# More rooms for prefetched expert weights, two output-projection chunks loaded early in both layers, and the recurrence's tables ordered behind the first norm

## The chip, the cores and the metric

The kernel runs on one core of a Trainium2 chip. The metric is the device time of one execution in microseconds (us); lower is better. Engines are called by the profile's short names: PE (TensorE), PEld (its weight loads), DVE (VectorE), ACT (ScalarE), POOL (GpSimd) and SP (SyncE, which here issues almost all loads).

## The reference, cut to what matters

Two layers over 512 tokens of width 1024: 256 latent tokens and 256 context tokens. Only the latent tokens are needed at the end, so layer 1 computes its queries, merge and experts for 256 tokens.

```python
h = modulate(rms_norm(x), shift, scale)        # shift, scale, gate = (silu(c) @ ada_w + ada_b)
parts = project(h, w_in)                       # attention, S5, HGRN, and 3*1024 gate logits
y_att, y_s5, y_hg = diff_attention, s5 recurrence, hgrn recurrence
g = sigmoid(gate_logits)                       # (3, 1024)
m = g[0]*(y_att @ w_o_att) + g[1]*(y_s5 @ w_o_s5) + g[2]*(y_hg @ w_o_hg)
x = x + gate1 * (m @ w_out)
h2 = modulate(rms_norm(x))
x = x + gate2 * hier_moe(h2)                   # 32 experts, top 2 in one of 4 groups
# one expert: (silu(xb @ w_gate[e]) * (xb @ w_up[e])) @ w_down[e]
```

An S5 recurrence needs tables, powers of its complex decay, that depend on the weights alone.

## The kernel before, in words

Each layer has three stages, and one scheduler (it keeps a model of the engines' time and fixes, before the run, the order of instructions on each engine) puts them in order.

**Dense** (`dense`): the norm and its modulation (`norm_mod`, lines L332 to L344) write the transposed activations as two parts `hTh` and `hTl`; `w_in` comes in chunks of 1 MB (`wchunk`, L159, tiles `wst`), each is split by ACT (`wh`, L364) and DVE (`wl`, L367), and a product is three matmuls (L347 to L349). Results go to DRAM: the gates as `dg` (12 blocks), the branches' outputs as `dy`. In layer 0 the stage begins with the modulation vector: `ada_step` (L264) multiplies chunks of `ada_w` into `adaP`, `ada_end` adds a bias on DVE (L270, `stg`), turns the result on PE (L273) and copies it to `mod` (L276), which the norm's modulation needs. `s5_prep` computes the S5 tables (tiles `p_a`, `p_b`, `p_w`, `p_e`, `p_cu`, `p_u`, `p_t`, `p_pw`; L213 to L218 are the complex multiplication `cmul`, L563 to L565 the drive table), mostly on DVE; L584 and L596 are the S5 matmuls on PE that use them.

**Merge**: for each branch the output comes back from DRAM (`yf`, L1299), is split (`yh` on ACT, L729, `yl` on DVE, L730), and is multiplied by its `w_o` chunk in four column blocks; each block is multiplied by its gate (`gt`, L1316, from `dg`) and added up in `mTl`. S5 comes first, HGRN second, attention last. Then `w_out` in four chunks, c = 0 to 3, each a column block: the product, `m_w` (L1351, times the gate), and the add to `Xx`/`Xctx` (L1354), and the router's share of those columns. In both layers w_out's chunks come through the four rooms `wp`, which the `w_o` chunks hold before; in layer 1 the chunks 2 and 3 go to two of the rooms `xw` instead (the list `Wo`).

**Experts** (`expert_rows`): 32 experts in 192 chunks of 1 MB per layer (`mgate`, `mup`, `mdown`: 64 each), always in one order. Each chunk takes the next room of a list, `self.slots`: the `xw` rooms (7 in layer 0, 11 in layer 1, in the space that `hTh` and `hTl` leave), the 4 `wp`, and the rooms `xt` (4 in each layer, one of them in layer 0 opened late as `NXU`). `prefetch` (L189) issues the load on SP; where it is called in merge, a one-element DVE copy (L184) into the room ties it to a step: `PM` says how many follow each of merge's 12 column blocks, `PF` how many follow the first `m_w` of each w_out chunk, `PRE` how many before the router's count is read back. SP then reads that count (`v_n`, L1769) and branches (L1770). In layer 0 a pass computes two experts for two token halves (12 chunks, 16 groups); in layer 1 four experts (24 chunks, 8 groups). `pg`, `pu`, `py` are the three products (L1627); `cw` (L1753, DVE) weights a result and POOL adds it to the tokens (L1755).

All loads on SP's queue are issued in order: an item whose room is not free holds back those behind it.

Of the kernel before, what the change touches and what calls it, by code (L numbers as in the profile page):

```python
# [13 lines left out]
OP = mybir.AluOpType  # L14
# [6 lines left out]
LEVELS = (64, 32, 16, 8, 4, 2, 1)  # L21
SCAN_ORD = list(range(31, -1, -1)) + list(range(63, 31, -1))
NE = 32
NXW = (7,11)
NXT = (4,4)
PRE = (3,0)
NXU = (1,0)
ORDER = ((0, 8, 9, 7, 10, 11, 1), (0, 8, 9, 7, 10, 11, 1))
SHARE = (0, 3)
ATT1 = (0, 0)  # L30
PM = ((0,0,0,0,0,0,1,1,1,1,1,0),(0,0,0,0,0,0,0,0,1,1,1,1))
PF = ((0,0,1,2),(2,3,3,0))

ROWS = 32

# [91 lines left out]
class Trunk:  # L127
# [35 lines left out]
    def stream_begin(self, l):  # L163
        self.nxw = NXW[l]
        self.xw = self.mes.enter_context(self.tc.tile_pool(name=f"mw{l}", bufs=self.nxw, side="right"))
# [159 lines left out]
    def norm_mod(self, l, Z, R, hi, lo, pool):  # L325

        nc = self.nc
        g = pool.tile([128, 8], FT, name="nmg")
        nc.scalar.dma_start(g, self.h["nmix"][l])
        a = pool.tile([128, 8, 2], FT, name="nma")  # L330
        m = self.mod[l]
        nc.vector.scalar_tensor_tensor(a, m[:, 8:16, :], 1.0, g[:, :, None].to_broadcast([128, 8, 2]), op0=OP.add, op1=OP.mult)  # L332
        for j in range(8):
            T = Z[:, j]
            if R is not None:
                T = pool.tile([128, 512], FT, name="nzr", bufs=2)
                nc.vector.tensor_mul(T, Z[:, j], R)
            f = pool.tile([128, 512], FT, name="nf", bufs=2)
            nc.scalar.activation(f[:, 0:256], T[:, 0:256], AF.Identity, bias=m[:, j, 1:2], scale=a[:, j, 1:2])
            nc.vector.tensor_scalar(f[:, 256:512], T[:, 256:512], a[:, j, 0:1], m[:, j, 0:1], op0=OP.mult, op1=OP.add)  # L340
            nc.scalar.copy(hi[:, j, :], f)  # L341
            (nc.gpsimd if j % 2 else nc.vector).tensor_sub(lo[:, j, :], f, hi[:, j, :].bitcast(FT))


# [153 lines left out]
    def s5_prep(self, l, ps, ne):  # L498

        nc, tc, h = self.nc, self.tc, self.h  # L500
        V, G = nc.vector, nc.gpsimd
        store = (nc.sync if l == 0 else nc.scalar).dma_start
        with ExitStack() as es:
# [5 lines left out]
            nc.sync.dma_start(dd, h["s5d"][l])  # L509
            if l == 0:  # L510
                yield from self.s5_setup(pool)
            else:
                yield
            T = self.s5t[l]
            C, P, F = self.s5s[l]

# [559 lines left out]
    def dense(self, l):  # L1076
        nc, tc, h = self.nc, self.tc, self.h
# [4 lines left out]
        es = ExitStack()  # L1082
# [20 lines left out]
        if l == 0:  # L1103
            self.cond_vectors(ap)
            self.s5k = ap
            with ExitStack() as ns:
                npool = ns.enter_context(tc.tile_pool(name=f"nrm{l}", bufs=1))
                X = npool.tile([128, 4, D], FT, name="nx")
                ada = self.ada(0, 0, ap)
                next(ada)  # L1110
                for t in range(NT):
                    nc.sync.dma_start(X[:, t], h["x" if t > 1 else "ctx"][128 * (t % 2):128 * (t % 2) + 128])
                next(ada)
                pre = self.s5_prep(l, ps, 2)
                next(pre)
                with tc.high_priority():
                    turned = self.norm_rows(l, [X[:, t] for t in range(NT)], npool, acc)
                    for _ in ada:
                        pass
                    self.norm_mod(l, *turned, hi, lo, npool)  # L1120
                for _ in pre:
                    pass
        if l == 0:
            def rest():
                for a, g in ((0, 1), (0, 2), (1, 0), (1, 1), (1, 2)):
# [118 lines left out]
        pre = self.s5_prep(1, ps, 1) if l == 0 else iter(())  # L1244
# [31 lines left out]
        ls.close()  # L1276
        clear()

        Wo = {c: self.wchunk(h["w_out"][l, c], self.xw) for c in ((2, 3) if l else ())}
        self.slots = self.slots[len(Wo):] + self.slots[:len(Wo)]  # L1280
        with ExitStack() as ss:
            mp = ss.enter_context(tc.tile_pool(name=f"mrh{l}", bufs=1))
# [5 lines left out]
            with ExitStack() as s2:  # L1288
                yp = s2.enter_context(tc.tile_pool(name=f"yp{l}", bufs=1, side="right" if l == 0 else "left"))
                yi = s2.enter_context(tc.tile_pool(name=f"yi{l}", bufs=2, side="right" if l == 0 else "left"))  # L1290
                for bi, (b, prs) in enumerate(((1, (2,)), (2, (3,)), (0, (0, 1)))):
                    Y, W = {}, {}
                    for p in prs:
                        if p == 2 and ys5:
                            Y[p] = [[t[:, k] for t in ys5] for k in range(2)]
                        else:
                            m = 1 if p == 1 and ya3 else 2
# [6 lines left out]
                    for q in range(4):  # L1304
# [29 lines left out]
                            nc.sync.dma_start(t, h[n].rearrange("(t p) d -> p t d", p=128))  # L1334
                        for _ in range(PM[l][4 * bi + q]):
                            self.prefetch(m_[:, 0] if one else m_)
            self.router_begin(l, ps, pa)
            for c in range(4):
                P = [bank() for _ in range(nq // 2)]
# [16 lines left out]
                        for _ in range(PF[l][c]):  # L1356
                            self.prefetch(w[:, 0])
                self.router_cols(l, c)
            while self.taken < self.nxw + 4:
                self.prefetch()  # L1360
            self.sp = [t for t in self.sp if t is self.sp0]
            with tc.high_priority():
# [5 lines left out]
    def router_begin(self, l, ps, pl):  # L1368

        nc, h = self.nc, self.h  # L1370
# [9 lines left out]

        rp = self.rp = self.rts.enter_context(self.tc.tile_pool(name=f"rt{l}", bufs=1, side="right"))
        rk = lambda nm, *sh: rp.tile([128, *sh], FT, name=nm)
        self.constants(rp, "route", nc.gpsimd)
        wr, br, gc = rk("r_w", 8, 36), rp.tile([1, 36], FT, name="r_b"), rk("r_g", 8)
        nc.sync.dma_start(wr, h["wr"][l])
        nc.sync.dma_start(br, h["br"][l:l + 1])
# [2 lines left out]
        m = self.mod[l]  # L1389
# [3 lines left out]
        for r in rs:  # L1393
            a = self.rc[r] = self.mp.tile([128, 8], FT, name=f"r_c{r}")
# [134 lines left out]
    def moe(self, l, rs):  # L1529
        nc, tc, h = self.nc, self.tc, self.h  # L1530
# [3 lines left out]
        es = ExitStack()  # L1534
# [9 lines left out]
        ng, m = NE // na, na * nq  # L1544
        self.g2 = {r: self.mod_bc(mp, l, 5, r, f"g2_{r}") for r in ((0, 1) if l == 0 else (0,))}

        xt = es.enter_context(tc.tile_pool(name=f"mx{l}", bufs=NXT[l] - NXU[l]))
        self.slots += [xt] * (NXT[l] - NXU[l])
        self.slots = self.slots[self.taken % len(self.slots):] + self.slots[:self.taken % len(self.slots)]
        for _ in range(PRE[l]):  # L1550
            self.prefetch()
# [10 lines left out]
            return OH  # L1562
        first = picked(0)
        self.router_rows(l, rs, 1)
        if NXU[l]:
            xt = es.enter_context(tc.tile_pool(name=f"my{l}", bufs=NXU[l]))
            self.slots = [xt] * NXU[l] + self.slots
        self.m2 = es.enter_context(tc.tile_pool(name=f"mo2{l}", bufs=2))
        self.ot = self.m2.tile([128, nt * 128], FR, name="ot", bufs=1)
        def gather(q, OH, part=None):  # L1570

# [11 lines left out]
        if l:  # L1583
            nxt = gather(0, first)
        for _ in range(NXT[l] - PRE[l]):
            self.prefetch(self.X[x0])
# [3 lines left out]
        for p in range(ng):  # L1590
# [18 lines left out]
            with self.in_order(), tc.high_priority() if last else nullcontext():  # L1609
                back = self.expert_rows(*cur[p % nq], na, self.ns, W, last, before, behind)  # L1610
                for f in back if last else ():
                    f()
        es.close()
        self.mes.close()

    @contextmanager
# [58 lines left out]
    def expert_rows(self, xT, sl, na, ns, W, last=False, before=lambda: None, behind=lambda: None, later=True):  # L1675
# [4 lines left out]
        nc = self.nc  # L1680
# [31 lines left out]
        for i, (c0, m) in enumerate(((0, 512), (512, 256), (768, 256)) if last else ((0, 512), (512, 512))):  # L1712
            n, c1 = divmod(c0, 512)
            cut = lambda t: t[:, 0:m]
            Y = cut(self.py.tile([128, 2, 256], FT, name="py").rearrange("p a n -> p (a n)"))
            for k in range(4):
                for a in range(ng):
                    self.pe(nc.tensor.matmul, Y[ps_[a]], hT[:, k, ps_[a]], part(W[4 + n][a % na], k)[:, c1:c1 + m], start=k == 0, stop=k == 3)
            whole = last and m < 512
            yh = cut(self.parts("wh", FT if whole else FR))  # L1720
            S.activation(yh, Y, AF.Identity, scale=sl[:, 0:1])  # L1721
            if not whole:
                yl = cut(self.parts("wl"))
                V.scalar_tensor_tensor(yl, Y, sl[:, 0:1], yh.bitcast(FT), op0=OP.mult, op1=OP.subtract)
            back.append(lambda c0=c0, m=m, yh=yh, yl=None if whole else yl, i=i: self.expert_back(c0, m, yh, yl, ns, last, i))
            if not later or last and i:
                back.pop(0)()
# [125 lines left out]
```

## Time and profile before

| | us |
|---|---|
| median of 3 runs | 2017.79 (2015.47 to 2020.94) |
| the profiled execution, its own time | 2008.41 |
| its span in the profile | 2006.7 |
| PE busy | 1745.2 (87%) |
| DVE busy | 1036.7 (52%) |
| ACT busy | 534.3 (27%) |
| POOL busy | 506.5 (25%) |
| mean granted TensorE clock | 0.947 |

The stages, by the start of their first matmuls: dense of layer 0 from 43, merge from 541.8, w_out about 590 to 647, router to 678, experts to about 1143; dense of layer 1 to about 1489 (its merge begins at about 1473), w_out 1497 to 1530, router, and experts from 1548.4 to the end. Shares of busy time over the whole span hide that the stages have different limits, so the stages are read one by one.

### The profile page before, as it was taken

What the parts mean: (1) busy time and instruction counts of PE and PEld (TensorE: products, weight loads), DVE (VectorE), ACT (ScalarE), POOL (GpSimd) and SP (SyncE); (2) the same over time, 40 slices, a digit from 0 to 9 for tenths busy, and PEclk for the clock granted to TensorE, in tenths of its full rate; (3) what the DMA queues carried; (4) which work ended last, traced back from release to release, by engine and by line L of the source; (5) the groups of instructions that cost most, each with busy time, mean ns of one, the idle gap of its engine ahead of it and who ended that gap; (6) DMA issues with size and microseconds to landing.
All of it is one profiled execution on the core that took longest, in us unless ns stands there. A gap on an engine that the chain in (4) does not pass through costs nothing. (4 is left out here: it accounts for less than half of the span.)

```text
span 2006.7 us, 31800 instructions
## 1 busy us (share of the span) xinstructions
PE 1745.2 (87%) x12480; PEld 1092.6 (54%) x12480; DVE 1036.7 (52%) x2354; ACT 534.3 (27%) x1002; POOL 506.5 (25%) x473
## 2 busy tenths in 40 slices
PE   4899999998999799999999899979987777776776
PEld 2867776775679443444343398878786222221222
DVE  7968757969674333443343448679875011110112
ACT  3233543432333211111111243465443100000000
POOL 1643133404220023332333422146420001010111
PEclk7999999998999899999999989989998988998898
DMA  8587575556892799999999756454379999999997
GB/s 326 182 270 227 212 298 195 183 202 225 299 347 102 292 418 418 419 419 419 419 418 419 289 165 206 153 197 175 98 280 367 416 420 420 419 420 420 420 420 286
DMA packets 172178, 615.89 MB, mean 307 GB/s; under 512 B 24789, under 2 KB 90453, under 8 KB 109045
## 3 DMA queue, kind: packets, MB, share of 16 engines
q1 hardware_dynamic: 146244, 579.96, 74.3%
q10 hardware_dynamic: 25680, 33.56, 4.9%
q8 instruction: 100, 1.64, 0.3%
q14 instruction: 58, 0.47, 0.1%
q0 software_dynamic: 96, 0.26, 0.0%
HBM read 573.15 MB, written 40.58 MB: 306 GB/s over the span
## 5 line engine op out<-in xcount | busy, mean ns | idle before, releaser
L1700 DVE TENSOR_TENSOR hd<-hd,pu 128x512 f32<-128x512 f32 x24 | 16.5, 688 | 597.9 <-PE pu L1627 597.9
L1627 PE MATMUL pu<-wst,xT 128*32 128x512 f32 x1536 | 223.6, 641 | 49.3 <-DMA wst<-mup 49.2
L1627 PE MATMUL pg<-wst,xT 128*32 128x512 f32 x1536 | 215.5, 622 | 51.8 <-DMA wst<-mgate 50.5
L367 DVE TENSOR_TENSOR wl<-wst,wh 128x512 fp32r<-128x512 f32 x240 | 193.6, 809 | 116.1 <-ACT wh L364 114.4
L1755 POOL TENSOR_TENSOR Xx<-Xx,cw 128x512 f32<-128x512 f32 x92 | 117.1, 1279 | 459.6 <-DVE cw L1753 459.5
L1627 PE MATMUL py<-wst,hd 128*32 128x512 f32 (+1 forms) x1600 | 196.5, 602 | 41.4 <-DMA wst<-mdown 23.8
L364 ACT CAST wh<-wst 128x512 fp32r<-128x512 f32 x256 | 157.2, 618 | 281.4 <-PE acc L349 104.2
L1755 POOL TENSOR_TENSOR Xctx<-Xctx,cw 128x512 f32<-128x512 f32 x64 | 81.9, 1280 | 398.6 <-DVE cw L1753 398.6
L347 PE MATMUL acc<-wh,hTh 128*128 128x256 f32 x528 | 162.2, 311 | 10.8 <-ACT hTh L341 6.6
L349 PE MATMUL acc<-hTh,wl 128*128 128x512 f32 (+1 forms) x480 | 168.5, 356 | 3.0 <-DVE wl L367 2.9
L348 PE MATMUL acc<-wl,hTh 128*128 128x256 f32 x528 | 163.1, 310 | 9.3 <-DVE wl L367 9.3
L347 PE MATMUL acc<-hTh,wh 128*128 128x512 f32 (+1 forms) x480 | 170.4, 356 | 0.3 <-ACT wh L364 0.3
L1627 PEld LDWEIGHTS pu<-wst,xT 128*32 128x32 f32 x1536 | 57.1, 116 | 208.2 <-issue 114.5
L348 PE MATMUL acc<-hTl,wh 128*128 128x512 f32 (+1 forms) x480 | 169.4, 353 | 0.0
L1627 PEld LDWEIGHTS pg<-wst,xT 128*32 128x32 f32 x1536 | 55.7, 114 | 201.4 <-issue 111.5
L349 PE MATMUL acc<-wh,hTl 128*128 128x256 f32 x528 | 159.1, 308 | 0.0
L1627 PEld LDWEIGHTS py<-wst,hd 128*32 128x32 f32 x1600 | 53.4, 114 | 170.8 <-issue 107.4
L1721 ACT ACTIVATE wh<-py,sl 128x512 fp32r<-128x512 f32 (+1 forms) x50 | 33.5, 670 | 368.4 <-PE py L1627 366.3
L347 PEld LDWEIGHTS acc<-wh,hTh 128*128 128x128 f32 x528 | 113.2, 216 | 19.2 <-ACT hTh L341 7.3
L348 PEld LDWEIGHTS acc<-wl,hTh 128*128 128x128 f32 x528 | 114.2, 217 | 13.3 <-DVE wl L367 10.5
L1753 DVE TENSOR_TENSOR cw<-py,g 128x512 f32<-128x512 f32 x160 | 105.4, 685 | 27.8 <-PE py L1627 14.1
L349 PEld LDWEIGHTS acc<-wh,hTl 128*128 128x128 f32 x528 | 112.5, 216 | 4.3 <-issue 3.1
(487 smaller groups left out, 3205.4 us busy)
## 6 DMA issues: line engine op xcount, KB each, us to landing
wst<-mgate SPq DMA_DIRECT2D x128, 1024.0 KB
wst<-mup SPq DMA_DIRECT2D x128, 1024.0 KB
wst<-mdown SPq DMA_DIRECT2D x122, 1024.0 KB
wst<-ada_w SPq DMA_DIRECT2D x48, 1024.0 KB
wst<-w_in SPq DMA_DIRECT2D x48, 1024.0 KB
wst<-w_o SPq DMA_DIRECT2D x8, 1024.0 KB
wst<-w_out SPq DMA_DIRECT2D x8, 1024.0 KB
dg<-stg ACTq DMA_DIRECT2D x15, 512.0 KB
```

Of the source, the lines that this page charges most:

```text
L347: nc.tensor.matmul(out, a[0], b[0], start=start, stop=False)
L348: nc.tensor.matmul(out, a[0], b[1], start=False, stop=False)
L349: nc.tensor.matmul(out, a[1], b[0], start=False, stop=stop)
L364: nc.scalar.copy(r(wh), s)
L367: e.tensor_sub(r(wl), s, r(wh).bitcast(FT))
L1627: i = fn(*args, **kw)
L1700: V.tensor_mul(hd, hd, P[1])
L1721: S.activation(yh, Y, AF.Identity, scale=sl[:, 0:1])
L1753: V.tensor_mul(w, cps[s], self.g2[1 if x0 + at < 2 else 0][:, None, cs].to_broadcast([128, nb, m]))
L1755: (V if nb > 1 and at + nb == nt else G).tensor_tensor(x, x, w, op=OP.add)
```

## The change

It does seven things; the arithmetic stays what it was.

1. Rooms. `NXW` goes from 7 and 11 to 9 and 13; a new pool `me` of `NXE` = 3 and 2 rooms opens on merge's end, when the space of `yf` and `gt` is free; `xt` goes from 4 and 4 to 2 and 3; `NXU` goes away. All in all 18 rooms instead of 15 in layer 0, and 22 instead of 19 in layer 1.
2. `PM`, `PF` and `PRE`: in layer 1, 7 chunks instead of 4 are loaded during merge; behind w_out's chunk c = 0 there are 8 and 9 instead of 0 and 2, and one behind each of the other three (before 0, 1, 2 and 3, 3, 0); then 2 and 3 instead of 3 and 0.
3. `Wo`, the early load of w_out's chunks 2 and 3 into `xw` rooms, now holds for layer 0 too.
4. The S5 tables from the second part on (`p_b`, `p_w`, `p_a`, `p_e` and what follows) are traced with an order: behind the third modulation on DVE (`self.normed`).
5. The router's constants (`cst_route`) are loaded on SP's queue and not on POOL's.
6. With 5, the scratch space for POOL's DMAs shrinks (`dynamic_dma_scratch_size=1024`).
7. In layer 0's experts a second pair of buffers for the split of `py` (`mos0`): the two output halves alternate.

```diff
-NXW = (7,11)
-NXT = (4,4)
-PRE = (3,0)
-NXU = (1,0)
+NXW = (9,13)
+NXE = (3,2)
+NXT = (2,3)
+PRE = (2,3)
-PM = ((0,0,0,0,0,0,1,1,1,1,1,0),(0,0,0,0,0,0,0,0,1,1,1,1))
-PF = ((0,0,1,2),(2,3,3,0))
+PM = ((0,0,0,0,0,0,1,1,1,1,1,0),(0,0,0,0,0,1,1,1,1,1,1,1))
+PF = ((8,1,1,1),(9,1,1,1))
...
-            nc.vector.tensor_scalar(f[:, 256:512], T[:, 256:512], a[:, j, 0:1], m[:, j, 0:1], op0=OP.mult, op1=OP.add)
+            v = nc.vector.tensor_scalar(f[:, 256:512], T[:, 256:512], a[:, j, 0:1], m[:, j, 0:1], op0=OP.mult, op1=OP.add)
             nc.scalar.copy(hi[:, j, :], f)
+            self.normed = v.ins if j < 3 else self.normed
...
             if l == 0:
                 yield from self.s5_setup(pool)
-            else:
-                yield
+            yield
...
-                for _ in pre:
-                    pass
+                next(pre)
+                with tc.issue_after(self.normed):
+                    for _ in pre:
+                        pass
...
-        Wo = {c: self.wchunk(h["w_out"][l, c], self.xw) for c in ((2, 3) if l else ())}
+        Wo = {c: self.wchunk(h["w_out"][l, c], self.xw) for c in (2, 3)}
...
+            xe = self.mes.enter_context(tc.tile_pool(name=f"me{l}", bufs=NXE[l], side="right"))
+            at = self.nxw - len(Wo) - self.taken
+            self.slots = self.slots[:at] + [xe] * NXE[l] + self.slots[at:]
             self.router_begin(l, ps, pa)
...
-            while self.taken < self.nxw + 4:
+            while self.taken < self.nxw + NXE[l] + 4:
                 self.prefetch()
...
-        self.constants(rp, "route", nc.gpsimd)
+        self.constants(rp, "route", nc.sync)
...
-        xt = es.enter_context(tc.tile_pool(name=f"mx{l}", bufs=NXT[l] - NXU[l]))
-        self.slots += [xt] * (NXT[l] - NXU[l])
+        xt = es.enter_context(tc.tile_pool(name=f"mx{l}", bufs=NXT[l]))
+        self.slots += [xt] * NXT[l]
...
-        if NXU[l]:
-            xt = es.enter_context(tc.tile_pool(name=f"my{l}", bufs=NXU[l]))
-            self.slots = [xt] * NXU[l] + self.slots
+        if l == 0:
+            self.sp.append(es.enter_context(tc.tile_pool(name=f"mos{l}", bufs=1)))
...
+            self.sp.append(self.sp.pop(0))
             yh = cut(self.parts("wh", FT if whole else FR))
...
-    nc = bacc.Bacc("TRN2", target_bir_lowering=False, num_devices=1)
+    nc = bacc.Bacc("TRN2", target_bir_lowering=False, num_devices=1, dynamic_dma_scratch_size=1024)
```

What this does to the order of instructions is shown at three places. Line numbers of the changed kernel are 1 to 7 higher than those of the kernel before.

SP's queue at the passage from dense to merge in layer 0, before (`w_o` are the three branches' output weights, `yf` a branch's output, `gt` a gate block):

```order
136 L159 DMA wst<-w_o 128x2048 x3
137 L1299 DMA yf<-dy_797 128x2x512
138 L1316 DMA gt<-dg_4_789 128x2x512
139 L1316 DMA gt<-dg_5_790 128x2x512
140 L1316 DMA gt<-dg_6_791 128x2x512
141 L159 DMA wst<-w_o 128x2048
142 L1299 DMA yf<-dy_797 128x2x512
143 L1316 DMA gt<-dg_7_792 128x2x512
144 L159 DMA wst<-w_out 128x2048
```

and with the change:

```order
140 L160 DMA wst<-w_o 128x2048 x4
141 L160 DMA wst<-w_out 128x2048 x2
142 L1302 DMA yf<-dy_797 128x2x512
143 L1319 DMA gt<-dg_4_789 128x2x512
144 L1319 DMA gt<-dg_5_790 128x2x512
145 L1319 DMA gt<-dg_6_791 128x2x512
146 L1302 DMA yf<-dy_797 128x2x512
147 L1319 DMA gt<-dg_7_792 128x2x512
148 L160 DMA wst<-w_out 128x2048
```

The fourth `w_o` chunk and two w_out chunks now stand ahead of the first `yf`. The first of these w_out chunks goes to an `xw` room, whose space is that of `hTh`: it waits for the last dense matmul that reads `hTh`. The second waits, besides, until the fourth `w_o` has landed.

SP's queue in layer 1, from merge's last loads on, before:

```order
362 L159 DMA wst<-w_out 128x2048
...
367 L159 DMA wst<-w_out 128x2048
368 L1316 DMA gt<-dg_2_10764 128x2x256
369 L1316 DMA gt<-dg_3_10765 128x2x256
370 L159 DMA wst<-w_out 128x2048 x2
371 L189 DMA wst<-mgate 128x2048 x3
372 L1385 DMA r_w<-wr 128x288
...
375 L189 DMA wst<-mgate 128x2048 x5
376 L189 DMA wst<-mup 128x2048 x7
377 L1769 TENSOR_LOAD v_n
```

and with the change:

```order
363 L160 DMA wst<-w_out 128x2048
...
370 L160 DMA wst<-w_out 128x2048 x2
371 L190 DMA wst<-mgate 128x2048 x6
372 L155 DMA cst_route<-cst_route 128x256
373 L1391 DMA r_w<-wr 128x288
374 L190 DMA wst<-mgate 128x2048
...
377 L160 DMA wst<-w_out 128x2048
378 L190 DMA wst<-mgate 128x2048
379 L190 DMA wst<-mup 128x2048 x8
380 L190 DMA wst<-mdown 128x2048 x6
381 L1776 TENSOR_LOAD v_n
```

The load of w_out's chunk 1 (367 before, 377 now) moved behind chunks 2 and 3 and seven expert chunks. It now waits for the ACT cast of the last quarter of chunk 0, whose room it takes: the three other `wp` rooms go to expert chunks. Before the count is read (`TENSOR_LOAD`) there are 22 expert loads and not 15. In layer 0 the same load moved in the same way: there it waits for the DVE split of the last quarter of chunk 0.

DVE at the start of layer 0, around the bias add of the modulation vector (`stg`), before:

```order
138 L215 TENSOR_TENSOR p_cu<-p_u_423,p_u_424 128x32
139 L215 TENSOR_TENSOR p_b<-p_a_504,p_a_505 128x16x2
140 L216 TENSOR_TENSOR p_u_423<-p_cu 128x32
141 L217 TENSOR_TENSOR p_u_424<-p_cu 128x32
142 L216 TENSOR_TENSOR p_a_504<-p_b,p_cu 128x16x2
143 L217 TENSOR_TENSOR p_a_505<-p_w,p_cu 128x16x2
144 L270 TENSOR_TENSOR stg<-adaP,adab 128x512
```

and with the change:

```order
131 L218 TENSOR_TENSOR p_u_424<-p_cu 128x32
132 L219 TENSOR_TENSOR p_cu<-p_u_423,p_u_424 128x32
133 L214 TENSOR_TENSOR p_u_423<-p_cu 128x32
134 L215 TENSOR_TENSOR p_u_424<-p_cu 128x32
135 L271 TENSOR_TENSOR stg<-adaP,adab 128x512
...
141 L215 TENSOR_TENSOR p_u_424<-p_cu 128x32
142 L216 TENSOR_TENSOR p_cu<-p_u_423,p_u_424 128x32
143 L277 COPY mod_103<-adaP 128x32
```

Only the short chain of `p_cu` and `p_u` still stands ahead of `stg`; the tables `p_a`, `p_b`, `p_w` and `p_e` come behind the modulation.

## Rows read from the trace of the kernel before

**Rows 1.** The page: busy time by engine, and loads in 40 slices of 50.2 us.

```profile
PE 1745.2 (87%) x12480; PEld 1092.6 (54%) x12480; DVE 1036.7 (52%) x2354; ACT 534.3 (27%) x1002; POOL 506.5 (25%) x473
...
GB/s 326 182 270 227 212 298 195 183 202 225 299 347 102 292 418 418 419 419 419 419 418 419 289 165 206 153 197 175 98 280 367 416 420 420 419 420 420 420 420 286
```

**Rows 2.** PE's waits by line, 28 to 541 us: total us, times, longest.

```profile
PE oth L596 <- DVE p_w L578: 10.0, 6, 3.6
PE adaP L273 <- DVE stg L270: 5.1, 2, 4.7
...
PE oth L584 <- DVE p_e L565: 3.6, 2, 3.2
```

**Rows 3.** PE's waits by line, 700 to 1130 us.

```profile
PE py L1627 <- DVE cw L1753: 16.6, 15, 1.7
PE pu L1627 <- DMA wst<-mup: 1.4, 1, 1.4
```

**Rows 4.** Windows: us, busy PE PEld DVE ACT POOL, clock, DMA share, GB/s.

```profile
541.00:560.00 19.00, 18.03 (x79) 14.55 (x79) 13.06 (x19) 7.03 (x11) 1.78 (x2) 1.00 1.02 372
657.00:664.00 7.00, 2.28 (x9) 2.15 (x10) 5.77 (x29) 1.91 (x5) 0.00 (x0) 0.50 1.02 427
664.00:670.00 6.00, 6.00 (x30) 5.42 (x29) 0.30 (x2) 0.00 (x0) 0.00 (x0) 0.53 0.20 81
1491.00:1556.00 65.00, 52.57 (x417) 45.40 (x419) 39.90 (x131) 24.69 (x55) 0.58 (x1) 0.87 0.90 357
1600.00:1650.00 50.00, 35.59 (x208) 12.19 (x208) 8.20 (x20) 3.77 (x7) 5.01 (x4) 0.92 1.01 420
```

**Rows 5.** The page: the chain that ended last.

```profile
DMA wst<-mdown 7%; DMA wst<-mup 7%; DMA wst<-mgate 7%; PE py L1627 0%; PE pg L1627 0%; PE pu L1627 0%; PE py L1625 0%; SPq L189 0%; DVE cw L1753 0%; DVE Xx L1755 0%; PE pt L1625 0%; DVEq L1753 0%
```

**Rows 6.** PE's timeline at the start: start us, duration, instruction, idle before.

```profile
31.36 1.94 PE L264 MATMUL adaP<-wst,ca 128*32 128x512 f32 x8 [0.56 <-DMA wst<-ada_w]
...
43.17 0.60 PE L347 MATMUL acc<-wh,hTh 128*128 128x256 f32 x1 [4.08 <-ACT hTh L341]
```

**Rows 7.** DVE's timeline at the start.

```profile
34.16 1.14 DVE L218 TENSOR_TENSOR p_w<-p_a,p_a 128x16 f32<-128x16 f32 x1
...
37.23 0.69 DVE L270 TENSOR_TENSOR stg<-adaP,adab 128x512 f32<-128x512 f32 x1
```

**Rows 8.** SP's timeline where dense of layer 0 ends.

```profile
528.67 1.19 SPq L159 DMA_DIRECT2D wst<-w_o  x2
530.16 0.74 SPq L1299 DMA_DIRECT2D yf<-dy  x1
530.95 3.62 SPq L1316 DMA_DIRECT2D gt<-dg  x3
```

**Rows 9.** PE's timeline, merge's first matmul in layer 0.

```profile
541.79 0.73 PE L347 MATMUL oth<-yh,wh 128*128 128x512 f32 x2 [0.70 <-ACT yh L729]
```

**Rows 10.** ACT's timeline there.

```profile
540.69 1.05 ACT L729 CAST yh<-yf 128x1024 fp32r<-128x1024 f32 x1 [2.39 <-DMA gt<-dg]
```

**Rows 11.** PE's waits by line, 541 to 600 us.

```profile
PE acc L347 <- DVE gt L1325: 2.6, 2, 1.7
```

**Rows 12.** DVE's timeline at w_out's chunk 0 in layer 0.

```profile
599.43 0.69 DVE L367 TENSOR_TENSOR wl<-wst,wh 128x512 fp32r<-128x512 f32 x1 [2.07 <-ACT wh L364]
600.88 1.41 DVE L1351 TENSOR_TENSOR m_w<-acc,g 128x512 f32<-128x512 f32 x2 [0.76 <-PE acc L349]
```

**Rows 13.** SP's timeline from merge to experts in layer 1.

```profile
1477.61 0.35 SPq L159 DMA_DIRECT2D wst<-w_out  x1
...
1489.45 0.82 SPq L159 DMA_DIRECT2D wst<-w_out  x2
...
1543.07 12.71 SPq L189 DMA_DIRECT2D wst<-mdown  x8
```

**Rows 14.** DVE's timeline, the end of w_out's chunk 0 in layer 1.

```profile
1506.71 0.68 DVE L1351 TENSOR_TENSOR m_w<-acc,g 128x512 f32<-128x512 f32 x1
```

**Rows 15.** PE's timeline, the first expert product of layer 1.

```profile
1548.36 4.93 PE L1627 MATMUL pg<-wst,xT 128*32 128x512 f32 x44
```

More of the change, by code (lines that the diff above doesn't have):

```diff
@@ L1613, in moe @@
         es.close()
+        self.sp = [self.sp0]
         self.mes.close()
```

## The prediction

> **What bounds the kernel now.** I read the page first: PE is busy 87% of the span and the bytes per second differ by a factor of four from stage to stage [rows 1], so I went stage by stage with the table of waits. In dense of layer 0 PE waits little: for the modulation vector at the start, and for S5 tables [rows 2]. In the experts of layer 0 PE waits 16.6 us for `cw` and once, 1.4 us, for a load [rows 3]: PE sets the pace there, the loads just keep up. In the experts of layer 1 the loads set it: 420 GB/s without a gap [rows 4], and the chain that ended last is made of expert chunks, 7% each of `mdown`, `mup`, `mgate` [rows 5]. A chunk of 1.049 MB takes 2.50 us there. So time in the first three quarters is lost or won on PE; at the end it is lost or won on idle time of the loads.
>
> A median of 2017.8 us stands against the profiled execution's 2008.4, 0.5% less. My sum is of differences, and I add it to the median. 0.3%, or 6 us, is what a measurement of this kernel can tell from no change.
>
> **The start: -4.5 us.** `adaP` is done at 33.3 (31.36 + 1.94) [rows 6], but `stg` on DVE begins at 37.23, behind table work such as `p_w` at 34.16, 1.14 us long [rows 7]. PE waits 4.7 of its 5.1 us on `stg` there [rows 2], and the first product begins at 43.17 [rows 6]. With the change only `p_cu` and `p_u`, short operations, stand ahead of `stg` and `mod`. That gives back at most 5.1 us, at least 0 if the chain's next link (a norm not turned yet) is late; I take 4.5, since `stg` waits 3.9 us behind the tables and the modulation too is freed of them. It is kept afterwards, since PE has almost no other idle time up to merge.
>
> The tables themselves come some 6 us later. PE waits 13.6 us for `p_w` and `p_e` as it is [rows 2]. The changed order puts more products ahead of the first S5 matmul on PE, so I cost this at nothing; if that cover is too short it is a rival below.
>
> **Merge in layer 0: +10 us, and +3 us of clock.** Before, SP issues two `w_o` at 528.67, the first `yf` at 530.16, three `gt` from 530.95, all while PE still works on dense [rows 8]. The cast of `yf` begins at 540.69 and PE's first merge matmul at 541.79, after a wait of 0.7 us [rows 9, 10]. With the change the two w_out chunks stand ahead of `yf` on SP. The first of them takes a room in the space of `hTh`, so it can't go before the last dense matmul, which ends at 541.1 before (541.79 less the wait of 0.70, [rows 9]) and at 536 to 537 after the start's gain. From 536 the same amount has to come as before: two chunks, `yf`, three `gt`. Before, that took from 528.67 to 540.69, 12.0 us. So `yf` is in at 548, and PE begins at 549.2 with the cast's 1.05 us, a wait of 13.2 us in place of 0.7: 12.5 us. Some comes back: loads are near their limit through this merge (372 GB/s, [rows 4]), only one of the two chunks is really an addition (the other takes the place of a load that moves behind w_out's chunk 0), and PE's later waits there, above all 2.6 us for `gt` [rows 11], can shrink. I take 10, bounds 2.5 (one chunk more, all else hidden) and 13.
>
> Were the loads on SP's queue served strictly one after another, `yf` would be through after 2.5 chunks, 2.6 MB at 372 GB/s or 7 us, and PE would begin at 545, 4 us sooner. The row speaks against it: with two chunks ahead, `yf` of half a chunk took 10.5 us from its issue, about as long as the `gt` behind it [rows 8, 10]. The Trainium skill, "DMA: Bandwidth & Descriptors", section "Queues, rings and completion order", says that each DMA engine takes a queue's descriptors in ring order, with completion not in order. By it the sum below is 2026 instead of 2030.
>
> What such a wait does to the clock shows before the experts of layer 0: after a stretch in which PE had 2.28 us of work in 7, at clock 0.50, PE is busy for 6.00 us in a row at 0.53, the lower level of 1.2 GHz, before it is back at 2.4 [rows 4]. Six microseconds at half speed lose 3; bounds 0 and 4.
>
> **w_out's chunk 1 in layer 0: +2.5 us.** Its load now waits for the split of the last quarter of chunk 0, at 599.43 [rows 12], and needs 2.5 us and some latency, 603 to 604, while PE has finished chunk 0 at 600.9 (`m_w`). Bounds 0 and 5. Chunks 2 and 3 are in place.
>
> **Experts in layer 0: -1.4 us.** Before the count is read 18 loads are issued instead of 14 (the fifteenth room opened later): up to 4 x 2.5 = 10 us of loads sooner, but only one wait of 1.4 us was for a load. The second split buffer lets `wl` of the second half go before two `cw`, but the wait of 16.6 us is for the `cw` of the next group's last products, and its place in the order is as before. Bounds -10 and +1. `cst_route` on SP: nothing, as it stands between loads that aren't waited for; bound 1.
>
> **Layer 1: +3 us.** Before, w_out's chunk 1 is issued at 1477.61, the chunks 2 and 3 at 1489.45 [rows 13]; PE finishes chunk 0 before 1506.71 (`m_w`) [rows 14]. With the change chunk 1 stands behind chunks 2 and 3 and seven `mgate`: with 1.5 us from issue to data (an estimate), nine chunks take 22.5 us from 1491, itself 2.5: it lands at 1516. PE wants it at 1506, and waits 10 us; then the clock, 3 us. The experts begin 13 us later than 1548.36 [rows 15], at 1561.4.
> Now the loads. From 1491 to 1556 they moved 357 x 65 = 23.2 MB [rows 4], 55.2 us at 420: 9.8 us idle, part of it waiting for the count, after which SP issues on at 1543.07 [rows 13]. With the change 25 chunks can go from 1491 on without a stop (2 + 7 + 1 of w_out + 12 + 3), 62.4 us, to 1554 or 1555 with the small tables. Then every room is full until the first half of `pg` is through, 32 matmuls at 4.93 / 44 us [rows 15] or 3.6 us after 1561.4: 10 us idle. So idle time is as before, plus 2.5 us for the w_out chunk that used to come earlier: +3. Were chunk 1 in time, there would be no idle time: -9.8 + 2.5 = -7.3. With 5 us more of a wait: +8.
>
> **Sum:** -4.5 + 10 + 3 + 2.5 - 1.4 + 3 = +12.6 us: 2017.8 + 12.6 = 2030.
>
> **Rivals.**
> *Faster: the loads of layer 1 never stop.* Place: w_out's chunk 1 in layer 1. If it lands by 1509, less than 3.5 us late, then 22 expert chunks are in when `pg` begins and rooms come free as the last one lands: -7.3. For it: the loads were idle 9.8 us there, and the 9 chunks ahead of it may be issued later than I think, so that it shares the queue with fewer. Together with a merge loss of 4 and no clock lost in layer 0: -4.5 + 4 + 1 - 1.4 - 7.3 = -8.2, 2010. Against it: the order on SP is fixed, and its room comes free late in any case. Chance 0.30.
> *No difference:* layer 1 gains so, but merge in layer 0 loses as forecast: -4.5 + 10 + 3 + 2.5 - 1.4 - 7.3 = +2.3, 2020. Chance 0.16.
> *Ring order:* as forecast, with merge cheaper by 4: 2026. Chance 0.14.
> *The tables come too late:* PE waits at its first S5 matmuls for the 6 us: 2036. For it: those waits are there already [rows 2]. Chance 0.10.
> That more rooms don't fit or aren't used is no rival: the order on SP shows 22 loads.
>
> **How the numbers follow.** The forecast has 0.30. Slower by over 0.3% are it, ring order and the tables: 0.54; within 0.3%: 0.16; faster: 0.30. The range, 2003 to 2042, reaches below the faster case by 7 (the start's and the experts' bounds) and above the forecast by 12 (13 instead of 10 in merge, 5 more in layer 1, the tables); 0.1 is left out at each end.
>
> **What would show it.** Right: `stg` at 33.5 and the first product at 38; in merge of layer 0 one wait of PE of 8 us or more for `yh`, with a lower clock behind it; a wait of some 10 us for w_out's chunk 1 (`wh`) in layer 1; a gap in the loads around 1555 to 1565, plus the shift of layer 0. Wrong: `yf` in within 4 us of dense's end, or loads in layer 1 at 420 GB/s from 1491 to the end.

## The result, and the profile after

The changed kernel takes 2032.9 us (median of 4 runs, 2026.2 to 2036.0) against 2016.6 (4 runs, 2011.1 to 2020.9): a ratio of 1.0075, 95% interval 1.0051 to 1.0099, slower by about 15 us. Its profiled execution has a span of 2024.4 us, 17.7 more than that of the kernel before.

Where it went, by marks that both traces have (us from the span's start):

| mark | before | after | later by | step adds |
|---|---|---|---|---|
| first product on PE | 43.2 | 40.6 | -2.5 | -2.5 |
| last dense matmul of layer 0 ends | 541.1 | 546.3 | 5.2 | +7.7 |
| first merge matmul, layer 0 | 541.8 | 558.9 | 17.1 | +11.9 |
| first `m_w` of w_out's chunk 0 | 600.9 | 616.5 | 15.7 | -1.5 |
| first `pg`, layer 0 | 677.8 | 698.0 | 20.2 | +4.6 |
| norm of layer 1 (`ndg` on PE) | 1155.6 | 1172.7 | 17.1 | -3.1 |
| SP issues w_out's chunks 2 and 3, layer 1 | 1489.5 | 1504.7 | 15.2 | -1.9 |
| `m_w` of chunk 0, layer 1 | 1506.7 | 1520.4 | 13.7 | -1.6 |
| `m_w` of chunk 1, layer 1 | 1511.8 | 1544.7 | 32.9 | +19.2 |
| first `pg`, layer 1 | 1548.4 | 1578.4 | 30.1 | -2.8 |
| last matmul ends | 2001.9 | 2019.4 | 17.5 | -12.6 |

**The start.** PE's timeline of the changed kernel (start, duration, instruction, idle before it):

```profile
31.48 1.06 PE L265 MATMUL adaP<-wst,ca 128*32 128x512 f32 x8 [1.42 <-DMA wst<-ada_w]
36.57 1.12 PE L274 MATMUL adaP<-cst_all,stg 128*128 128x128 f32 x4 [4.02 <-DVE stg L271]
40.63 0.60 PE L349 MATMUL acc<-wh,hTh 128*128 128x256 f32 x1 [2.95 <-ACT hTh L342]
```

and DVE's there:

```profile
33.07 0.30 DVE L219 TENSOR_TENSOR p_cu<-p_u,p_u 128x32 f32<-128x32 f32 x1
...
35.73 0.18 DVE L215 TENSOR_TENSOR p_u<-p_cu 128x32 f32<-128x32 f32 x1
35.83 0.68 DVE L271 TENSOR_TENSOR stg<-adaP,adab 128x512 f32<-128x512 f32 x1
```

`adaP` is done at 32.5 (31.48 + 1.06), 0.8 us sooner than before, and `stg` starts at 35.83 instead of 37.23 [rows 7]. So `stg` still stands 3.3 us behind the short chain of `p_cu`, where it stood 3.9 us behind the tables. The start wins 2.5 us [rows 6]: 0.8 on `adaP`, 0.6 on the wait of `stg`, and 1.1 between `stg` and the first product.

**The rest of dense, layer 0.** Dense ends 7.7 us later than its start would have it. PE's timeline of the changed kernel has one long wait there that the kernel before does not have, and the windows (columns as in [rows 4]) show the clock behind it:

```profile
306.13 2.07 PE L877 MATMUL oth<-h_q,h_kx 64*128 64x128 f32 x8 [6.12 <-DVE h_S L825]
```

```profile
300.00:310.00 10.00, 3.88 (x13) 2.94 (x12) 10.00 (x21) 6.16 (x8) 4.57 (x5) 0.63 0.37 128
310.00:320.00 10.00, 10.00 (x39) 6.84 (x39) 6.09 (x16) 2.44 (x4) 0.89 (x1) 0.68 0.40 120
```

`h_S` belongs to HGRN. DVE writes it at 305.5, 20.1 us later than before (285.4). PE stands still for 6.1 us, until that instruction of DVE is done (the trace puts the release of the matmul down to it), and then runs at the lower of its two clock levels until about 316.2, which costs some 5 us more (half of 10). Part of this is made up elsewhere in dense. All six runs with the tables' order have this wait (5.7 to 6.1 us), and none of the five without it.

**Merge of layer 0.** PE's, SP's and ACT's timelines, in this order:

```profile
541.97 1.07 PE L597 MATMUL oth<-cst_all,p_w 128*128 128x128 f32 x8 [1.20 <-DVE p_kk L591]
558.91 0.80 PE L349 MATMUL acc<-yh,wh 128*128 128x512 f32 x1 [12.21 <-ACT yh L730]
```

```profile
547.65 0.81 SPq L160 DMA_DIRECT2D wst<-w_out  x2
548.90 0.38 SPq L1302 DMA_DIRECT2D yf<-dy  x1
549.33 1.68 SPq L1319 DMA_DIRECT2D gt<-dg  x3
```

```profile
545.34 0.36 ACTq L600 DMA_DIRECT2D win<-p_wo  x1
...
557.82 1.04 ACT L730 CAST yh<-yf 128x1024 fp32r<-128x1024 f32 x1 [10.41 <-DMA yf<-dy]
```

The forecast wait is there, 12.2 us instead of 0.7 [rows 9], with `yf` behind two w_out chunks, 18.7 us later than before [rows 8]. But there is a second thing: the last S5 matmul of the layer-1 tables (L597) runs at 541.97, and the last store that follows from it, `win`, goes out at 545.34. In the kernel before (PE's timeline, then ACT's) both came some 18 us sooner, ahead of `yf`:

```profile
524.70 0.60 PE L596 MATMUL oth<-cst_all,p_w 128*128 128x128 f32 x4
```

```profile
527.04 0.33 ACTq L599 DMA_DIRECT2D win<-p_wo  x1
```

**w_out's chunk 1, layer 0.** SP's timeline of the changed kernel, ACT's, and windows (columns as in [rows 4]):

```profile
609.63 0.33 SPq L160 DMA_DIRECT2D wst<-w_out  x1
```

```profile
621.26 1.66 ACT L366 CAST wh<-wst 128x512 fp32r<-128x512 f32 x3
```

```profile
609.60:614.00 4.40, 4.30 (x53) 4.13 (x52) 1.21 (x9) 0.00 (x0) 0.00 (x0) 1.00 0.69 246
614.00:618.00 4.00, 3.57 (x39) 3.22 (x34) 1.86 (x5) 0.00 (x0) 0.00 (x0) 1.00 0.01 6
617.00:622.00 5.00, 2.68 (x15) 1.77 (x13) 3.51 (x15) 3.15 (x11) 0.00 (x0) 0.81 0.45 143
622.00:627.00 5.00, 5.00 (x25) 5.00 (x25) 1.81 (x3) 0.92 (x2) 0.00 (x0) 0.50 1.00 423
627.00:632.00 5.00, 5.00 (x31) 5.00 (x31) 0.69 (x1) 0.62 (x1) 0.00 (x0) 0.66 1.02 423
```

The load goes out at 609.63. In the next 4.4 us 1.08 MB come (246 GB/s), then the loads all but stop: chunk 1 is in by about 614, 3 us before PE ends chunk 0's products at 617.2. So nobody waits for the load. But in ACT's order and in PE's, the router's work on chunk 0's columns now stands ahead of chunk 1: ACT casts it at 621.26, and PE waits 1.0, 0.6 and 0.7 us for `Xctx`, `Xx` and `r_hT`. It has 2.68 us of work in 5, and is then busy at the lower clock until about 630. Before, it went from chunk 0 straight to chunk 1 at full clock. From the `m_w` of chunk 0 to that of chunk 1 it takes 21.8 us instead of 16.4; 0.8 us of this come back up to `pg`, which leaves the 4.6 us.

**Layer 1.** SP's timeline, then PE's, ACT's, DVE's:

```profile
1504.67 0.82 SPq L160 DMA_DIRECT2D wst<-w_out  x2
1505.59 10.34 SPq L190 DMA_DIRECT2D wst<-mgate  x6
1516.24 0.33 SPq L155 DMA_DIRECT2D cst_route<-cst_route  x1
1518.16 0.33 SPq L1391 DMA_DIRECT2D r_w<-wr  x1
...
1526.89 0.33 SPq L160 DMA_DIRECT2D wst<-w_out  x1
```

```profile
1530.48 1.12 PE L1405 MATMUL att<-r_w,mod 128*1 128x36 f32 x16 [7.99 <-DMA r_w<-wr]
...
1535.77 0.58 PE L349 MATMUL acc<-wh,mTh 128*128 128x256 f32 x1 [0.32 <-ACT wh L366]
```

```profile
1535.10 1.66 ACT L366 CAST wh<-wst 128x512 fp32r<-128x512 f32 x3 [12.01 <-DMA wst<-w_out]
```

```profile
1520.36 0.69 DVE L1357 TENSOR_TENSOR m_w<-acc,g 128x512 f32<-128x512 f32 x1 [2.19 <-PE acc L351]
...
1544.70 0.69 DVE L1357 TENSOR_TENSOR m_w<-acc,g 128x512 f32<-128x512 f32 x1
```

Chunk 1 goes out 22 us after the chunks 2 and 3, behind seven `mgate` and the router's tables. ACT waits for it until 1535.10, and PE begins its products at 1535.77. PE's own wait in the meantime, 7.99 us, is for `r_w`, which stands behind six `mgate` on the same queue and ahead of chunk 1 in PE's order. The windows show what the loads do:

```profile
1505.00:1571.00 66.00, 43.54 (x318) 41.04 (x317) 37.81 (x121) 21.78 (x49) 0.00 (x0) 0.80 1.00 408
1571.00:1583.00 12.00, 10.10 (x80) 6.96 (x84) 3.43 (x16) 3.01 (x5) 0.00 (x0) 0.80 0.06 24
```

They run full until about 1571 and then all but stop for 12 us: all rooms are full, and the first one comes free behind `pg`, at 1578.42 + 3.5. By then 22 chunks are in, and of the 30.1 us that `pg` is late 12.6 come back by the end.

### The profile page after: what moved, and what is told of

Read it like the earlier page. It is cut to its first block, busy times and chain, and to the rows that moved or that the text cites. A ratio compares the mean times of both kernels' runs of the same rounds, so it can differ in the third digit from the quotient of the medians.

```text
span 2024.4 us, 31840 instructions
## 1 busy us (share of the span) xinstructions
PE 1742.8 (86%) x12480; PEld 1098.9 (54%) x12480; DVE 1041.1 (51%) x2364; ACT 535.4 (26%) x1002; POOL 497.5 (25%) x471
## 5 line engine op out<-in xcount | busy, mean ns | idle before, releaser
L1728 ACT ACTIVATE wh<-py,sl 128x512 fp32r<-128x512 f32 (+1 forms) x50 | 33.5, 670 | 297.7 <-PE py L1633 293.3
```

## The experiments

Each span and each mark below is of one profiled execution, and those scatter by some 5 us from run to run: three kernels below with one and the same dense stage end it at 542.0, 545.5 and 545.7. The verdicts go by the ratio of the runs to those of the kernel before on the same chip.

### w_out's early chunks of layer 0 behind merge's loads

```diff
-        Wo = {c: self.wchunk(h["w_out"][l, c], self.xw) for c in (2, 3)}
-        self.slots = self.slots[len(Wo):] + self.slots[:len(Wo)]
+        Wo = {}
+        def early():
+            Wo.update({c: self.wchunk(h["w_out"][l, c], self.xw) for c in (2, 3)})
+            self.slots = self.slots[2:] + self.slots[:2]
+        if l:
+            early()
...
+            if l == 0:
+                early()
             xe = self.mes.enter_context(tc.tile_pool(name=f"me{l}", bufs=NXE[l], side="right"))
```

> The changed kernel, but in layer 0 w_out's chunks 2 and 3 are loaded (into the same rooms) behind merge's own loads and not ahead of them. Theory (order on SP's queue): the wait of 12.2 us for yh at merge's start falls to 1 or less, and the low clock behind it goes; the kernel takes 9 to 12 us less than the changed one's 2024.4 span, about 2013. Rival (merge is limited by the loads as a whole): the wait moves to the later yf and gt of the same merge, gain 3 us or less.

Measured: 2023.1 us, ratio 1.0045 (1.0028 to 1.0062). PE's timeline and SP's waits (us in total, times, longest) of this run:

```profile
543.03 1.07 PE L597 MATMUL oth<-cst_all,p_w 128*128 128x128 f32 x8 [1.20 <-DVE p_kk L591]
...
554.69 0.80 PE L349 MATMUL acc<-yh,wh 128*128 128x512 f32 x1 [6.93 <-ACT yh L730]
```

```profile
SPq L1307 <- DMA win<-p_wo: 8.7, 3, 7.9
```

Neither the theory nor the rival: against the changed kernel's 1.0075 it is some 6 us better. Dense ends at 547.3 and merge begins at 554.7, with a wait of 6.9 us and no w_out load ahead of `yf`. SP holds `yf` for 7.9 us until the `win` stores have landed. So about 5 us of the wait are the w_out chunks' (with them ahead of `yf` and the tables' order in place it is 11.9 to 12.2 us in four runs), and the larger part is something else that makes `yf` late.

### The tables' order undone

```diff
-                next(pre)
-                with tc.issue_after(self.normed):
-                    for _ in pre:
-                        pass
+                for _ in pre:
+                    pass
```

(and the `yield` behind the setup, as in the kernel before)

> The changed kernel without the order that puts the S5 tables behind the third modulation on DVE. Theory (the later tables cost dense of layer 0 its 8 us): the first product comes back to about 43 us from 40.6, dense ends near 541 instead of 546.7, so 5 to 6 us less in all, about 2019 of span. Rival (dense is longer because the scheduler placed other things differently, not because of the tables): dense still ends at 546 or later, and the kernel is 0 to 3 us slower than the changed one.

Measured: 2018.9 us, ratio 1.0022 (1.0008 to 1.0036), better than the changed kernel's 1.0075 by about 11 us. The first product is at 43.25, dense ends at 543.2, merge begins at 543.7. SP's timeline:

```profile
532.28 0.72 SPq L1301 DMA_DIRECT2D yf<-dy  x1
...
543.26 0.82 SPq L160 DMA_DIRECT2D wst<-w_out  x2
```

The last L598 is at 526.83 and `yf` goes out at 532.28, ahead of the w_out chunks, which are traced in the same place as in the changed kernel. So their place ahead of `yf` in the changed kernel comes with the tables' order; that the scheduler put them there because `yf` had become late is the likely reason, but no run shows its reason. PE's wait at `h_S` is gone too. The theory holds and is larger than it said: the order costs dense's end and merge's wait.

### The order alone, in the kernel before

```diff
-                for _ in pre:
-                    pass
+                next(pre)
+                with tc.issue_after(self.normed):
+                    for _ in pre:
+                        pass
```

(and `self.normed`, and the `yield` behind the setup, as in the change)

> The kernel before with one part of the change alone: the S5 tables of layer 0 ordered behind the third modulation on DVE. Theory (the order makes S5, then HGRN, then the tables of layer 1 late, and yf's room waits for these): the first product at about 40.7 us, but HGRN's last output some 18 us later, dense ends 5 to 8 us later than 541.1, and PE waits 6 to 8 us for the first yf though no w_out load stands ahead of it; merge begins 10 to 14 us later than 541.8; span 2015 to 2021. Rival (the lateness of HGRN comes from the other parts of the change, the order is harmless): merge begins 0 to 4 us earlier than 541.8, span 2002 to 2007.

Measured: 2023.1 us, ratio 1.0041 (1.0019 to 1.0062): slower by 8 us by this part alone. PE's waits and SP's:

```profile
PE acc L348 <- ACT yh L729: 7.1, 1, 7.1
```

```profile
SPq L1301 <- DMA win<-p_wo: 8.7, 2, 8.2
```

Dense ends at 551.3, merge begins at 558.8 after 7.1 us of waiting, with no w_out chunk in front; the wait at `h_S` is there too, 5.7 us. Merge begins 17 us later than before, more than the 10 to 14 of the theory. The chain can be followed in the traces by its first and last pieces (us; "order undone" is the run above):

| piece | before | the order alone | changed kernel | order undone |
|---|---|---|---|---|
| first S5 scan work on DVE | 141.8 | 159.7 | 156.5 | 142.3 |
| last S5 work on DVE | 226.8 | 237.3 | 234.1 | 227.3 |
| HGRN's first output store | 439.9 | 463.9 | 458.9 | 442.3 |
| last S5 matmul of layer 1's tables | 524.7 | 547.0 | 542.0 | 526.8 |

The layer-1 tables lie in the space that HGRN leaves: DVE's timeline of the changed kernel shows them start with HGRN's store,

```profile
461.90 0.07 DVE L519 MEMSET p_b<- 128x16 f32 x1 [0.64 <-DMA dy<-h]
```

at 461.9 against 443.8 before. So the order delays S5, HGRN and the tables of layer 1, which cost PE nothing as long as it has products to do; at `h_S` it stands still for 6.1 us, and merge then waits for the last of them. The delay is not the same all along: in the changed kernel 14.7 us at S5's start, 7.3 at its end, 19.0 at HGRN's first output. Why HGRN loses more than S5's end no run shows.

### w_out's chunk 1 early

```diff
+            for c in (0, 1):
+                Wo[c] = self.wchunk(h["w_out"][l, c])
             self.router_begin(l, ps, pa)
             for c in range(4):
```

> The changed kernel with w_out's chunks 0 and 1 taken from their rooms ahead of the expert chunks behind them, in both layers, so that chunk 1 takes the room of a w_o chunk again and is loaded early. Theory (the late chunk 1 is what costs): layer 0 wins its 5.4 us after w_out's chunk 0; in layer 1 the 24 us between the m_w of chunks 0 and 1 fall to about 8 to 14 (the router's weights r_w still stand behind six expert chunks), experts start 10 to 18 us earlier, the gap of 11 us in the loads at 1571 to 1583 shrinks; in all 10 to 16 us less, span 2008 to 2014. Rival (the end is set by the sum of the loads alone): only layer 0's 5 us, span 2019.

Measured: 2018.7 us, ratio 1.0018 (0.9996 to 1.0039), better than the changed kernel by about 11 us. Chunk 1 takes a `w_o` room again. DVE's timeline in layer 1:

```profile
1521.73 0.69 DVE L1359 TENSOR_TENSOR m_w<-acc,g 128x512 f32<-128x512 f32 x1 [0.16 <-PE acc L351]
1527.80 0.69 DVE L1359 TENSOR_TENSOR m_w<-acc,g 128x512 f32<-128x512 f32 x1 [0.29 <-PE acc L351]
```

6.1 us between the two instead of 24.3: `r_w` is waited for no longer, because PE has chunk 1 to do meanwhile. The first `pg` of layer 1 moves from 1578.4 to 1563.7, the end from 2019.4 to 2011.7; in layer 0, from merge's first matmul to the first `pg`, 134.6 us instead of 139.1.

### Without the second pair of split buffers

```diff
-        if l == 0:
-            self.sp.append(es.enter_context(tc.tile_pool(name=f"mos{l}", bufs=1)))
...
-            self.sp.append(self.sp.pop(0))
```

> The changed kernel without the second pair of split buffers in the experts of layer 0. Theory (the 5.9 us that the experts of layer 0 won come from the loads being further ahead): that stage still takes about 461 us, span within 2 of 2024.4. Rival (they come from the second pair of buffers): the stage goes back to about 467 us, span 2029 to 2031.

Measured: 2031.9 us, ratio 1.0084 (1.0064 to 1.0103), the same as the changed kernel. From the first `pg` to the norm of layer 1 it takes 475.1 us, the changed kernel 474.6. The buffers do nothing that can be measured.

### Both repairs, and all three

The tables' order undone and chunk 1 early; then (`early`) also the w_out chunks of layer 0 behind merge's loads.

```diff
-                with tc.issue_after(self.normed):
...
+            if l == 0:
+                early()
...
+            for c in (0, 1):
+                Wo[c] = self.wchunk(h["w_out"][l, c])
```

(`early` and its call stand in the second of the two kernels alone)

> The changed kernel without the tables' order and with w_out's chunks 0 and 1 taken from their rooms ahead of the expert chunks. Theory (two separate costs that add): the 11 us of each alone come together, span about 2003 (2024 less 9 and less 11), faster than the kernel before by 5 to 10 us. Rival (both remove the same wait): span 2012 to 2015.

> As the run with no order and chunk 1 early, and besides w_out's chunks 2 and 3 of layer 0 loaded behind merge's loads. Theory: without the tables' order the first yf stands ahead of these chunks anyway, so only the second yf's wait behind them is left to win, 0 to 4 us: span 1999 to 2003. Rival (w_out's place on the queue is what counts, whatever the tables do): 5 us or more.

Measured: 2004.8 us, ratio 0.9941 (0.9920 to 0.9962), and 2005.6 us, ratio 0.9947 (0.9926 to 0.9967). The two repairs add up, and the third adds nothing that can be measured in the whole time. In merge of layer 0 it does show: from merge's first matmul to the first `m_w` it takes 64.6 us with the w_out chunks ahead of the second `yf`, and 59.1 with them behind, as in the kernel before (59.1). So these two chunks cost merge some 5 us there too. The first of the two kernels beats both the changed one and the one before, the latter by 12 us or 0.6%. A window of it in layer 1:

```profile
1491.00:1556.00 65.00, 53.16 (x437) 45.19 (x439) 40.24 (x132) 26.86 (x56) 0.00 (x0) 0.89 0.99 402
```

402 GB/s from 1491 to 1556, where the kernel before had 357 [rows 4].

### Fewer rooms

As the better kernel, without the pool `me`: 15 rooms in layer 0 and 20 in layer 1.

```diff
-NXE = (3,2)
+NXE = (0,0)
...
-PF = ((8,1,1,1),(9,1,1,1))
+PF = ((5,1,1,1),(7,1,1,1))
...
-            xe = self.mes.enter_context(tc.tile_pool(name=f"me{l}", bufs=NXE[l], side="right"))
```

> The kernel of the run with no order and chunk 1 early, but without the pool me: 15 rooms in layer 0 and 20 in layer 1, with 5 and 7 chunks behind w_out's chunk 0. Theory (the rooms are what wins in both expert stages): experts of layer 0 take 2 to 4 us longer than its 461.6, since loads are needed from further back, and in layer 1 two chunks fewer are in when pg begins, up to 5 us; span 2004 to 2009. Rival (the rooms are worth nothing, the gain over the kernel before is the order of loads alone): within 2 us of 1999.9.

Measured: 2009.6 us, ratio 0.9979 (0.9966 to 0.9992), against 0.9941 (0.9920 to 0.9962): the rooms are worth about 0.4%, with intervals that nearly touch. In layer 0 it takes 481.7 us from the first `pg` to the norm of layer 1, with the rooms 474.9. PE's timeline of this run, in the last group:

```profile
1130.05 3.63 PE L1631 MATMUL pu<-wst,xT 128*32 128x512 f32 x30 [1.35 <-DMA wst<-mup]
```

From the third group to the last but one, every group takes the same 28.55 or 29.36 us with 15 and with 18 rooms. From the last but one to the last (first `pu` to first `pu`) it takes 28.3 us with 15 rooms and 25.6 with 18, and from there to the norm 42.6 and 38.4. The one wait for a load is 1.35 us of this; what the rest is was not tried. In layer 1, from SP's w_out chunks 2 and 3 to the end, it takes 503.6 us with 20 rooms and 504.9 with 22: nothing. So the theory holds in layer 0, where the loss is larger than its 2 to 4 us and only in part a wait for loads, and the rival in layer 1.

### The order behind `stg` instead of the norm

```diff
-                with tc.issue_after(self.normed):
+                with tc.issue_after(self.first_stg):
```

(in the changed kernel with chunk 1 early; `first_stg` is the bias add of the first modulation)

> As the run with no order and chunk 1 early, but with the tables of layer 0 ordered on DVE behind the bias add stg and not behind the third modulation. Theory (what delays S5, HGRN and the tables of layer 1 is that table work moves from a stretch in which DVE has nothing else into one in which it shares with the splits wl): the tables start at about 36.5 instead of 31.7 or 40, so S5's scan starts some 5 us later than 141.8, and merge's first wait is 3 to 6 us; first product about 41.5, span 2001 to 2008. Rival (any such order makes the chain late, by way of the scheduler): merge begins at 555 or later, span 2012 to 2017, as with chunk 1 early alone.

Measured: 2023.1 us, ratio 1.0041 (1.0027 to 1.0056). Merge begins at 564.4 after a wait of 12.0 us, and S5's scan at 161.1; with the order behind the norm and chunk 1 early it was 561.1 and 157.9. The start is a miss of its own: the tables now stand between `stg` and `mod`, and the first product comes at 45.0, not at the 41.5 expected (40.3 with the order behind the norm). The rival holds: a weaker order makes the chain just as late. Why an order that moves the tables by 6 to 14 us (first `p_e` at 37.3 here, 43.8 in the changed kernel and 45.2 with the order alone, 31.7 before) makes S5's scan begin 15 to 19 us later stays open: between 100 and 140 us the changed kernel's DVE is busy for 27.0 us against 22.2 before, so more work falls there, but the scheduler's order changes as a whole with it, and no run separates the two.

## Why the prediction was right or wrong

Time and sign were right: 2030 forecast as slower by 12.6, measured 2032.9, slower by about 15 (17.5 in the profile). Part of the way there was not, and that the total comes so near is partly luck: 7.7 us in dense that the forecast had at nothing stand against 4.5 too many behind merge's start. Of its signs, the wait for `yh` with a lower clock behind it and the gap in the loads came; `stg` at 33.5 and the first product at 38 did not (35.8 and 40.6).

- **The start, -4.5:** -2.5. Failed: that with only "short operations" ahead of `stg` nearly all of its 3.9 us behind the tables come back. They are short, but each `p_cu` waits for the one before it, and together they hold `stg` back by 3.3 us.
- **The tables' lateness, costed at nothing "since the changed order puts more products ahead of the first S5 matmul":** this is the step that failed. The cover was there for layer 0's own S5 matmuls (PE waits 9.7 us at them up to 130, before 10.5), but I did not follow the chain behind them. S5, HGRN and layer 1's tables come 7 to 19 us later; PE waits 6.1 us until HGRN's `h_S` is written and then runs at the lower clock, dense ends 7.7 us later than its start allows, and the room of `yf` waits for the last stores of that chain. The rival had 6 us of waiting, but at the wrong place, and no part in merge.
- **Merge, +10 and +3:** measured +11.9 and then -1.5, with some 1.5 us of clock lost (granted 0.85 in the 10 us behind the wait, 1.00 in the next). The size of the wait was right, the cause half, so that size is luck: 5 us of the wait are the two w_out chunks, to which the forecast gave all of it, and 7 the tables. That a w_out chunk stands ahead of `yf` I read from the order as a cause of its own; without the tables' order `yf` goes first.
- **Ring order as a rival:** not decided. In the changed kernel `yf` was cast 10.2 us after the issue of the first w_out chunk, between the 7 of loads one after another and the 12.0 of the forecast. The 10.5 us by which the prediction spoke against the rival are no landing of `yf`: the row puts the end of that wait down to a `gt` [rows 10]. So no run here decides what the rule of the Trainium skill ("DMA: Bandwidth & Descriptors", "Queues, rings and completion order") would make of the time.
- **Chunk 1 in layer 0, +2.5:** +4.6 from `m_w` to `pg`. The wait for the load failed: chunk 1 was in 3 us before PE had ended chunk 0. What its late place on the queue changed is the order on ACT and PE, with the router's work ahead of chunk 1, and that costs waits of 2.3 us in all and the lower clock behind them; chunk 1 early takes this back.
- **Experts in layer 0, -1.4:** -3.1. From the first `pg` to the norm of layer 1 the eight runs with 18 rooms take 474.6 to 476.9 us, those with 15 rooms 477.7 (the kernel before), 481.7 and 482.0. Mis-sized: the one load that is late stands in the last group, and around it more is lost than the 1.4 us of the wait (2.6 of the 3.1 us lie between the first `pu` of the last group but one and that of the last); from 1060 to 1120 the kernel before was granted 0.97 of the clock, and the changed and the better kernel 1.00.
- **Layer 1, +3:** +2.3. The mechanism held: chunk 1 comes late (19.2 us between the two `m_w` beyond the 5.1 of before, forecast 13), the loads have their gap (12 us, forecast 10), and part comes back at the end. From the issue of chunks 2 and 3 it took 30.4 us until chunk 1 could be cast, and not 25: from 1504.67 to 1535.10 the loads moved 11.9 MB at 391 GB/s, where the forecast had ten chunks, 10.5 MB, at 420. Its 1.5 us from issue to data stand in no row; the loads reach 442 GB/s from 1507 on, 2.3 us behind that issue. SP also stood still for 11 us before chunk 1, waiting for earlier loads of its own queue; whether that delayed chunk 1 is not shown, since the loads ran on meanwhile. And were chunk 1 in time, -7.3 was forecast: with it early and no order, layer 1 takes 504.9 us from SP's w_out to the end, 512.5 before, -7.6. The five runs with chunk 1 early take 503.6 to 506.4, and the kernel before with the order alone 509.7, so the gain is 3 to 9 us.

## What to carry to other kernels

An order that is put on work beside the critical path has to be followed to the end of its chain: ask which buffers come free behind it, and what is loaded into them. Where a table shows a load ahead of another on a queue, ask first why, for that order may itself be a consequence of something that became late. And when rooms are handed to prefetches, take first the rooms for what is needed next: here one late chunk of 1 MB cost 11 us, and with it in its old place the additional rooms gained some 0.4%.

## What the runs showed of the hardware that was not expected

The price of a stall in clock differs from place to place. After 12.2 us without work before merge, PE was at the lower of its two levels (1.2 GHz) for 3.2 us of merge matmuls, from 558.9 to 562.1 (0.43 us from one to the next, then 0.23). After 6.1 us without work at `h_S` it was there for 10 us, from 306.1 to 316.2, with HGRN's matmuls on 64 rows, products, and `adaP` by turns (granted 0.50 up to 316). After w_out's chunk 0 in layer 0, where it had 2.68 us of work in 5, it was at the lower level for the whole of the next 5 us and about two thirds of the 5 after that (granted 0.50 and 0.66), while it did the router's matmuls and then products. What makes the difference was not tried.
